# Attention output projection of a hybrid encoder layer as two runs of eight output blocks, six of its 16 units by seven products

## The chip, the cores and the metric

The kernel runs on one core of one Trainium2 chip. The metric is the device time of one execution in microseconds (us), taken as the median of several runs. The engines are TensorE (PE in the profile; PEld is its loading of the stationary operand), VectorE (DVE), ScalarE (ACT), GpSimd (POOL, hardly used here) and SyncE (SP, whose queue issues the loads).

## The reference

One encoder layer over 256 tokens of width 2048, in float32. What matters here:

```python
n = rms_norm(h, norm_mix_w)
u = n @ w_in                  # latents | SSD z, xBC, dt_fwd, dt_bwd | g_attn, g_ssd
# attention: 16 heads, V_HEAD_DIM 128
p = softmax(scores * scale);  o = p @ v
attn_out = o.reshape(256, 2048) @ w_o_attn          # the output projection
# SSD: dt = softplus(dt_raw + dt_bias); a_cs = cumsum(-exp(a_log) * dt) in chunks of 128
mixed = sigmoid(g_attn) * attn_out + sigmoid(g_ssd) * ssd_out
h = h + mixed @ w_out
h = h + conv_ffn(rms_norm(h))
out = rms_norm(h)
```

## The kernel before

Every float32 product is made of three TensorE products: both operands are split into a rounded part and a rest (H and L), and HH, HL and LH are summed in PSUM.

Weights come in *units* of 16 blocks of 128x128, 1 MB. A unit is loaded into one of three raw buffers (`load`, L119), split in halves by ScalarE (`wh`, L195) and VectorE (`wl`, L196) into one of five pairs of buffers, and multiplied. `jobs` is the list of units in program order; `at(slot, fn)` hangs a smaller step, such as one step of an attention head, on the unit with that number. From this a scheduler fixes the order of the instructions on each engine; an instruction waits on semaphores for its inputs and for free buffers. Loads go out on SP's queue in the order of the units. Working tiles come from a pool of 29 pages (`page`) and one of 18 smaller ones (`p1`). PSUM has four banks for sums of units (`gpsum`, named g) and four for the rest (`spsum`, named s).

The stages that matter, in order:

- **Attention.** A string of letters gives the order of the units: R and V and QK for the heads, g for a unit of the attention's gate (`ga_job`). Each QK unit serves two heads, and each head then goes through `att1` (scores in PSUM, their maximum on VectorE L670, exponential on ScalarE L674, reciprocal and scaling of p on VectorE L676 and L678), `att2` (four transposes of p on TensorE, L686, copied into pT by ScalarE and VectorE) and `att3` (p times v, written as oT by L702 and L703). Fourteen of the 16 gate units stand here.
- **Output projection.** `quad` (L241) makes four units for each of four groups of four column blocks. A unit is 24 matmuls of 128x512 (L257, L258, L259), four loads of 256 KB, and two halves to split. At the end of a group `oa_evac` (L717) multiplies the gate with the sum straight from PSUM and the group is stored to `mixD`. The last two gate units stand between the first units, and the steps of dt (`dt_softplus` L495, `dt_tokens`, `dt_cumsum`, `dt_rows`) hang on slots 41 to 50 in this stage.
- **SSD start** and its eight groups, then the **SSD output projection**, which `os_run` (L921) does in two runs of eight column blocks with 16 units each. Four units of the first run and six of the second are *seven-product* units: a 2x2 block product by seven block products instead of eight (M1 to M7). Such a unit needs sums of weight blocks (`split_seven`, L152, on VectorE), sums of the left operand (`sums_of`, L892), and at the end of a run the combination of the seven sums (`inner` L939 and `outer` L950). M1, M5, M6 and M7 lie in s banks, the others in g banks.
- Output of the mixer and the convolutional MLP, which the change does not touch; the latter has its own seven-product units and calls `act_sums`.

Of the kernel before, what the change touches and what calls it, by code (L numbers as in the profile page):

```python
# [11 lines left out]
AF = mybir.ActivationFunctionType  # L12
ALU = mybir.AluOpType
AX = mybir.AxisListType

P = 128
# [48 lines left out]
def tile_bidir_hybrid_layer(ctx: ExitStack, tc, xT, pos, vec, cst, w_in, w_r, w_v, w_qk, w_oa,  # L65
# [11 lines left out]
    def page(shape, dt=F32, name="pg"):  # L77
        return pp.tile(shape, dt, tag="pg", bufs=NPG, name=name)
# [10 lines left out]
    def f32(ap):  # L89
        return ap.bitcast(F32)  # L90
# [150 lines left out]
    def quad(src, q, kt, get, evac):  # L241


        cell = {}

        def unit(u):
            def mm(h, n, wh, wl):
                if u == 0 and h == 0:
                    cell["ps"] = [gpsum([P, 512]), gpsum([P, 512])]
                wH, wL = (w.rearrange("p (k m) c -> p k (m c)", k=2) for w in (wh, wl))  # L250
                for kk in range(2):
                    k = 4 * u + 2 * h + kk
                    x = get(k)
                    for t in range(2):
                        ts = slice(t * P, (t + 1) * P)
                        ps = cell["ps"][t]
                        pe.matmul(ps, lhsT=x[:, 0, ts], rhs=wH[:, kk, :], start=k == 0, stop=False)  # L257
                        pe.matmul(ps, lhsT=x[:, 0, ts], rhs=wL[:, kk, :], start=False, stop=False)  # L258
                        pe.matmul(ps, lhsT=x[:, 1, ts], rhs=wH[:, kk, :], start=False, stop=k == kt - 1)  # L259

            def ev():
                if 4 * u + 4 == kt:
                    for t in range(2):
                        evac(q, t, cell["ps"][t])
            j = Job([src(4 * q + m)[:, 4 * u:4 * u + 4, :] for m in range(4)], 16, mm, ev)
            j.quad = True
            return j
        return [unit(u) for u in range(kt // 4)]
# [88 lines left out]
    def pair(st, k):  # L357
        return st[k // 2][:, :, k % 2, :]
# [333 lines left out]
    def att3(h):  # L692
        t = att.pop((h, "T"))
        vh, vl = vv[h // 4]
        d = slice((h % 4) * P, (h % 4) * P + P)
        ps = spsum([P, S])
        for kb in range(2):
            mm3(ps, vh[:, kb, d], vl[:, kb, d], t[:, 0, kb, :], t[:, 1, kb, :], kb == 0, kb == 1)
        if h % 2 == 0:
            oT[h // 2] = page([P, 2, 2, S], F32R, name="oT")  # L700
        o = oT[h // 2]
        act.activation(o[:, 0, h % 2, :], ps, AF.Copy)  # L702
        dve.tensor_sub(o[:, 1, h % 2, :], ps, f32(o[:, 0, h % 2, :]))  # L703


    ta, ts_ = {}, {}

    def gate_evac(store):
# [5 lines left out]

    mixD = dr.tile([4, P, 2, 512], F32, name="mixD")

    def oa_evac(q, t, ps):  # L717
        g = ta[q]
        dve.scalar_tensor_tensor(g[:, t, :], g[:, t, :], 1.0, ps, ALU.add, ALU.mult)
        if t == 1:  # L720
            nc.sync.dma_start(mixD[q], g)


    class Grp:
# [189 lines left out]
    def seven_left(pr, st, nm):  # L914
        if nm in ("A11", "A12", "A22"):
            k, t = int(nm[2]) - 1, int(nm[1]) - 1
            return [pr[:, i, k, t * P:(t + 1) * P] for i in range(2)]
        i = ("W1", "R", "N4", "N2").index(nm)
        return [a[:, i, :] for a in st]

    def os_run(n, order, cap):  # L921


        M, left, res = {}, {}, {}
        for kp, sv in order:
            for nm, c in ([(nm, 1) for hh in SEVEN for nm, _ in hh] if sv
                          else [(nm, 2) for nm in ("M2", "M3", "M4", "P22")]):
                left[nm] = left.get(nm, 0) + 3 * c
        total = dict(left)
        sevens_left = [sum(sv for _, sv in order)]  # L930

        def add(nm, aH, aL, bH, bL):
            if nm not in M:
                M[nm] = spsum([P, 512]) if nm in ("M1", "M5", "M6", "M7") else gpsum([P, 512])
            for x, w in ((aH, bH), (aH, bL), (aL, bH)):
                pe.matmul(M[nm], lhsT=x, rhs=w, start=left[nm] == total[nm], stop=left[nm] == 1)  # L936
                left[nm] -= 1

        def inner():  # L939
            c, v = page([P, 2, 512], name="m15"), page([P, 2, 512], name="vx")  # L940
            m1, m5, V, X = c[:, 0, :], c[:, 1, :], v[:, 0, :], v[:, 1, :]
            act.activation(m1, M["M1"], AF.Copy)
            act.activation(m5, M["M5"], AF.Copy)
            dve.tensor_sub(V, M["M6"], m1)
            dve.tensor_add(X, M["M7"], V)
            dve.tensor_add(V, V, m5)
            dve.tensor_add(m5, X, m5)
            res.update({(0, 0): m1, (1, 0): X, (0, 1): V, (1, 1): m5})

        def outer(h):  # L950
            for t, nm in ((0, ("M2", "M3")[h]), (1, ("M4", "P22")[h])):
                o = res[t, h]
                dve.tensor_tensor(o, M[nm], o, ALU.subtract if nm == "M4" else ALU.add)
            cap(n, h, res)

        def unit(i, kp, sv):
            def mm(h, nb, wh, wl):
                if sv:
                    for a, (nm, lf) in enumerate(SEVEN[h]):
                        aH, aL = seven_left(yHL[kp], yS[kp], lf)  # L960
                        add(nm, aH, aL, *(w[:, 4 * a:4 * a + 4, :].rearrange("p m c -> p (m c)")
                                          for w in (wh, wl)))
                else:
                    wH, wL = (w.rearrange("p (k m) c -> p k (m c)", k=2) for w in (wh, wl))
                    for k in range(2):
                        for t, nm in ((0, ("M2", "M3")[h]), (1, ("M4", "P22")[h])):
                            aH, aL = (yHL[kp][:, j, k, t * P:(t + 1) * P] for j in range(2))
                            add(nm, aH, aL, wH[:, k, :], wL[:, k, :])
                    if i == len(order) - 1:
                        outer(h)  # L970

            def ev():
                if sv:
                    sevens_left[0] -= 1
                    if sevens_left[0] == 0:
                        inner()
            kh, kk = kp // 8, 2 * kp % 16
            j = Job(w_os[8 * n:8 * n + 8, kh, :, kk:kk + 2, :].rearrange("m p k c -> p m (k c)"), 16, mm, ev)
            j.wide, j.seven = True, sv
            if sv:  # L980
                j.nh = 4
            return j
        assert not order[-1][1] and not order[0][1]
        return [unit(i, kp, sv) for i, (kp, sv) in enumerate(order)]
# [78 lines left out]
    def val_ev(m):  # L1063
        def ev(ps):
            o = conv3(ps, NFF + m)
            dve.tensor_mul(o, o, gv.pop(m))
            if m % 2 == 0:
                aHL[m // 2] = page([P, 2, 2, S], F32R, name="aHL")
            hi, lo = aHL[m // 2][:, 0, m % 2, :], aHL[m // 2][:, 1, m % 2, :]
            act.activation(hi, o, AF.Copy)  # L1070
            dve.tensor_sub(lo, o, f32(hi))  # L1071
            if m % 2 == 0:
                even[0] = o
            elif m // 2 in sevens:
                act_sums(m // 2, even[0], o)
        return ev


# [2 lines left out]
    NU = 5  # L1081
    sevens = {8 * p + u for p in range(2) for u in range(NU)}

    def act_sums(kp, e, o):
        w = page([P, 4, P], name="asum")
        sums_of([w[:, i, :] for i in range(4)], e, o)
        t = page([P, 2, 4, P], F32R, name="aS")
        hilo(t[:, 0], t[:, 1], w)
        aS[kp] = t[:, 0], t[:, 1]

    def seven_jobs(p):
        cell = {}
# [117 lines left out]
    def at(slot, fn, *a):  # L1210
        late.append((slot, lambda: fn(*a)))
# [24 lines left out]
    for m in range(7, 11):  # L1236
        at(m, rope_steps, 12 if m < 10 else 99)
    at(15, kr_rope)
    at(41, dt_softplus)
    at(46, dt_tokens)  # L1240
    at(48, dt_cumsum)
    at(50, dt_rows)

    ga = [0]
    ga_units = [u for q in range(4) for u in quad(lambda m: w_in[10 + m], q, 16, lambda k: pair(nHL, k),
# [4 lines left out]
    def ga_job():  # L1250
        jobs.append(ga_units[ga[0]])
        ga[0] += 1
# [33 lines left out]
            at(s + 3 + b, att2, 2 * i + b)  # L1286
            at(s + 4 + b, att3, 2 * i + b)

    for it in "g R0 g g g V0 QK0 g QK1 V1 QK2 g QK3 V2 R1 g QK4 g QK5 V3 QK6 g QK7 g g g g g".split():
        if it == "g":  # L1290
            ga_job()
        elif it[0] == "R":
            R(int(it[1]))
        elif it[0] == "V":
            Vj(int(it[1]))
        else:
            QK(int(it[2]))
    for q in range(4):
        for u in quad(lambda m: w_oa[m], q, 16, lambda k: pair(oT, k), oa_evac):
            jobs.append(u)  # L1300
            if ga[0] < 16:
                ga_job()
    gs = [0]

    def gate_s(n):
# [40 lines left out]
        at(b + i, ssd_sums, g)  # L1346
    for n in range(2):
        assert sorted(kp for kp, _ in runs[n]) == list(range(16))
        jobs += os_run(n, runs[n], cap)
    at(b + 17, ssd_r)  # L1350
    for q in range(2):
        at(b + 17 + q, mix_load, q)
# [245 lines left out]
```

## Time and profile before

| | us |
|---|---|
| median of 3 runs | 1944.09 |
| lowest and highest | 1944.06, 1944.98 |
| the profiled execution's own time | 1944.84 |
| its span, first to last instruction | 1943.1 |

| engine | busy us | share of the span | instructions |
|---|---|---|---|
| TensorE | 1928.8 | 99% | 10948 |
| VectorE | 1556.6 | 80% | 2583 |
| ScalarE | 1243.5 | 64% | 1975 |

A row of a group of instructions gives line, engine, operation, the tiles written and read, shapes and count, then busy time in us and the mean of one in ns, then the idle time ahead of it and what ended it. A row of the timeline gives start and duration in us, then the same names, and in square brackets the idle time before it. A row of a stretch gives the busy time of each engine in it with the number of its instructions, the clock that TensorE was granted (1.00 is full), and the share and rate of DMA. Attention's crowded part is 108 to 257 us, the output projection 257 to 363 us, the start of the SSD stage 363 to 435 us, the SSD output projection 935 to 1098 us.

### The profile page before, as it was taken

Reading aid. Unit: us, or ns where it says so; the run is one execution under the profiler, and the core shown is the slowest. Engines: PE = TensorE matmul, PEld = TensorE weight load, DVE = VectorE, ACT = ScalarE, POOL = GpSimd, SP = SyncE. Lnnn points to the kernel's source line nnn. Section 1 sums busy time; section 2 is a strip of 40 time slices with the busy share of each in tenths; the row PEclk is TensorE's granted clock in tenths of the full one; section 3 lists DMA queues with packets and bytes.
Section 4 is the critical chain, followed back from the end, with each engine's and each line's share of the span. In section 5 each row is a group of like instructions: output and inputs, shape, how many; then the busy total and the mean of one; then the engine's idle time right before and its main releaser. Section 6 shows DMA issues by size and latency. Waiting matters only on the chain.

```text
span 1943.1 us, 28860 instructions
## 1 busy us (share of the span) xinstructions
PE 1928.8 (99%) x10948; PEld 1689.8 (87%) x10948; DVE 1556.6 (80%) x2583; ACT 1243.5 (64%) x1975; POOL 16.2 (1%) x36
## 2 busy tenths in 40 slices
PE   9999999999999999999999999999999999999997
PEld 8899988888888888888888888888888888888887
DVE  7887765779779779779898876888887888977775
ACT  6566543788888887878665554665555565545563
POOL 0200000000000000000000000000000000000000
PEclk9999999999999999999999999999999999999998
DMA  7644456765665665665566675545555555564543
GB/s 283 203 158 159 131 174 218 252 225 174 217 220 173 214 233 168 208 237 170 172 198 204 209 256 176 193 177 197 183 185 217 177 205 182 182 209 179 206 163 125
DMA packets 118906, 379.55 MB, mean 195 GB/s; under 512 B 9712, under 2 KB 53168, under 8 KB 90864
## 3 DMA queue, kind: packets, MB, share of 16 engines
q1 hardware_dynamic: 116976, 375.09, 56.6%
q0 software_dynamic: 1024, 1.54, 0.3%
q8 instruction: 86, 1.41, 0.3%
q10 hardware_dynamic: 768, 1.09, 0.2%
q14 instruction: 52, 0.43, 0.1%
HBM read 372.08 MB, written 4.42 MB: 194 GB/s over the span
## 4 chain that ended last, share of the span: by engine, by line
PE 97%; DVE 1%; ACT 1%; DMA 1%; issue 0%; SPq 0%; DVEq 0%; ACTq 0%
PE g L222 41%; PE g L229 21%; PE g L936 7%; PE g L257 5%; PE g L258 4%; PE g L259 4%; PE s L936 1%; PE g L201 1%; PE g L203 1%; PE g L202 1%; PE s L222 1%; PE s L841 1%; PE s L850 1%; PE s L201 0%; PE s L203 0%; PE s L202 0%
## 5 line engine op out<-in xcount | busy, mean ns | idle before, releaser
L196 DVE TENSOR_TENSOR wl<-raw,wh 128x1024 fp32r<-128x1024 f32 (+1 forms) x634 | 754.5, 1201 | 207.4 <-ACT wh L195 127.7
L195 ACT ACTIVATE wh<-raw 128x1024 fp32r<-128x1024 f32 (+1 forms) x634 | 654.9, 1039 | 317.0 <-PE g L222 109.6
L222 PE MATMUL g<-xHL,wh 128*128 128x512 f32 x1424 | 341.7, 392 | 0.2 <-DVE cu L272 0.2
L222 PE MATMUL g<-hHL,wh 128*128 128x512 f32 x1408 | 327.8, 390 | 0.0
L222 PEld LDWEIGHTS g<-xHL,wh 128*128 128x128 f32 x1424 | 262.5, 188 | 52.1 <-PE s L203 0.4
L222 PEld LDWEIGHTS g<-hHL,wh 128*128 128x128 f32 x1408 | 261.4, 188 | 52.4
L229 PEld LDWEIGHTS g<-xHL,wl 128*128 128x128 f32 x1424 | 182.6, 191 | 6.9
L229 PE MATMUL g<-xHL,wl 128*128 128x256 f32 x1424 | 184.7, 283 | 0.0
L229 PEld LDWEIGHTS g<-hHL,wl 128*128 128x128 f32 x1408 | 174.8, 192 | 3.4
L229 PE MATMUL g<-hHL,wl 128*128 128x256 f32 x1408 | 176.0, 283 | 0.0
L1053 DVE SCALAR_TENSOR_TENSOR uc<-u,V,uc 128x255 f32<-128x255 f32 x176 | 84.6, 481 | 56.8 <-ACT uc L1051 55.3
L222 PE MATMUL g<-aHL,wh 128*128 128x512 f32 x532 | 126.8, 391 | 0.5 <-DVE aHL L1071 0.5
L1051 ACT ACTIVATE uc<-u,V 128x256 f32<-128x256 f32 x88 | 52.3, 594 | 116.5 <-DVE u L279 116.5
L936 PE MATMUL g<-wh,yHL 128*128 128x512 f32 x392 | 125.0, 390 | 0.0
L222 PEld LDWEIGHTS g<-aHL,wh 128*128 128x128 f32 x532 | 98.3, 188 | 20.8 <-DVE aHL L1071 1.4
L257 PE MATMUL g<-wh,xHL 128*128 128x512 f32 x256 | 100.3, 392 | 0.0
L258 PE MATMUL g<-wl,xHL 128*128 128x512 f32 x256 | 100.0, 390 | 0.0
L259 PE MATMUL g<-wh,xHL 128*128 128x512 f32 x256 | 99.6, 389 | 0.0
L936 PEld LDWEIGHTS g<-wh,yHL 128*128 128x128 f32 x392 | 73.6, 188 | 15.2
L147 ACT ACTIVATE wh<-raw 128x1024 fp32r<-128x1024 f32 (+1 forms) x80 | 56.9, 733 | 38.0 <-PE g L936 13.3
L936 PE MATMUL g<-wl,yHL 128*128 128x512 f32 x196 | 76.3, 389 | 0.0
L229 PEld LDWEIGHTS g<-aHL,wl 128*128 128x128 f32 x532 | 67.9, 191 | 2.4
(375 smaller groups left out, 2881.2 us busy)
## 6 DMA issues: line engine op xcount, KB each, us to landing
raw<-in_w_in SPq DMA_DIRECT2D x88, 1024.0 KB, 4.9
raw<-in_w_up SPq DMA_DIRECT2D x88, 1024.0 KB, 4.9
raw<-in_w_in SPq DMA_DIRECT2D x128, 256.0 KB, 3.8
raw<-in_w_os SPq DMA_DIRECT2D x32, 1024.0 KB, 6.0
raw<-in_w_dn SPq DMA_DIRECT2D x26, 1024.0 KB, 5.0
raw<-in_w_oa SPq DMA_DIRECT2D x64, 256.0 KB, 4.1
FB<-acsD SPq DMA_DIRECT2D x32, 512.0 KB, 7.5
raw<-in_w_out SPq DMA_DIRECT2D x12, 1024.0 KB, 5.0
```

The source lines that it names most:

```text
L147: act.activation(wh, v, AF.Copy)
L195: act.activation(vh, r, AF.Copy)
L196: dve.tensor_sub(vl, r, f32(vh))
L201: pe.matmul(ps, lhsT=wH, rhs=xH, start=first, stop=False)
L222: pe.matmul(ps, lhsT=wh[:, b, :], rhs=x, start=k == 0, stop=False)
L229: pe.matmul(cell["ps"][:, 0, :], lhsT=wl[:, b, :], rhs=get(k)[:, 0, :], start=False, stop=k == ktot - 1)
L257: pe.matmul(ps, lhsT=x[:, 0, ts], rhs=wH[:, kk, :], start=k == 0, stop=False)
L258: pe.matmul(ps, lhsT=x[:, 0, ts], rhs=wL[:, kk, :], start=False, stop=False)
L259: pe.matmul(ps, lhsT=x[:, 1, ts], rhs=wH[:, kk, :], start=False, stop=k == kt - 1)
L936: pe.matmul(M[nm], lhsT=x, rhs=w, start=left[nm] == total[nm], stop=left[nm] == 1)
L1051: act.activation(o, u, AF.Identity, scale=vcol("fcw", 88 + cb), bias=vcol("fcb", cb))
L1053: dve.scalar_tensor_tensor(o[:, a], u[:, b], vcol("fcw", k * 88 + cb), o[:, a], ALU.mult, ALU.add)
```

## The change

The output projection becomes two runs of eight column blocks with eight units each, by the function that the SSD output projection uses (`os_run`, now `mixed_run`, which takes the source of its weights and its left operands as arguments). In each run the units of head pairs 4, 5 and 6 are seven-product units: the order of a run is 0, S4, 1, S5, 2, S6, 3, 7. That makes 366 matmuls of 128x512 instead of 384, and 16 loads of 1 MB instead of 64 of 256 KB. For heads 8 to 13 `att3` first copies the PSUM tile into a page `of` by one more ScalarE step, and every second head VectorE adds up the four sums that the seven-product units need and splits them (`act_sums`). The end of a run is `inner`, two `outer`, and `oa_cap`, which multiplies the gates and stores two groups to `mixD`.

All 16 gate units now stand in the attention string, one more before V1 and one more before V3. `dt_softplus` hangs on slot 20, the V1 unit, instead of 41; the other dt steps on 36 to 38, at the end of the string.

```diff
+        if h // 2 in oa_sevens:
+            if h % 2 == 0:
+                of[h // 2] = page([P, 2, S], name="of")
+            f = of[h // 2][:, h % 2, :]
+            act.activation(f, ps, AF.Copy)
+        else:
+            f = ps
+        act.activation(o[:, 0, h % 2, :], f, AF.Copy)
+        dve.tensor_sub(o[:, 1, h % 2, :], f, f32(o[:, 0, h % 2, :]))
+        if h // 2 in oa_sevens and h % 2:
+            f = of.pop(h // 2)
+            act_sums(oS, h // 2, f[:, 0, :], f[:, 1, :])
+    oa_sevens, of, oS = {4, 5, 6}, {}, {}
...
-    def oa_evac(q, t, ps):
-        g = ta[q]
-        dve.scalar_tensor_tensor(g[:, t, :], g[:, t, :], 1.0, ps, ALU.add, ALU.mult)
-        if t == 1:
-            nc.sync.dma_start(mixD[q], g)
+    def oa_cap(n, h, res):
+        g = ta[2 * n + h]
+        for t in range(2):
+            dve.scalar_tensor_tensor(g[:, t, :], g[:, t, :], 1.0, res[t, h], ALU.add, ALU.mult)
+        nc.sync.dma_start(mixD[2 * n + h], g)
...
-    at(41, dt_softplus)
-    at(46, dt_tokens)
-    at(48, dt_cumsum)
-    at(50, dt_rows)
+    at(20, dt_softplus)
+    at(36, dt_tokens)
+    at(37, dt_cumsum)
+    at(38, dt_rows)
...
-    for it in "g R0 g g g V0 QK0 g QK1 V1 QK2 g QK3 V2 R1 g QK4 g QK5 V3 QK6 g QK7 g g g g g".split():
+    for it in "g R0 g g g V0 QK0 g QK1 g V1 QK2 g QK3 V2 R1 g QK4 g QK5 g V3 QK6 g QK7 g g g g g".split():
...
-    for q in range(4):
-        for u in quad(lambda m: w_oa[m], q, 16, lambda k: pair(oT, k), oa_evac):
-            jobs.append(u)
-            if ga[0] < 16:
-                ga_job()
+    order = [(int(w.lstrip("S")), w[0] == "S") for w in "0 S4 1 S5 2 S6 3 7".split()]
+    for n in range(2):
+        jobs += mixed_run(n, order, lambda m, k: w_oa[m:m + 8, :, k:k + 2, :].rearrange("m p k c -> p m (k c)"),
+                          oT, oS, oa_cap)
```

How the order of instructions moves, at three places on VectorE. Names of tiles: p, pT and oT are a head's tiles, sm its maxima and sums, s and g are PSUM banks, wl and vl low parts.

First, attention beside the units QK0 to QK2, behind the scaling of one head's p. Before:

```order
L678 TENSOR_SCALAR p<-p,sm 128x256 x2
L196 TENSOR_TENSOR wl<-raw,wh 128x4x2x128
L633 TENSOR_TENSOR vl<-g,vh 128x512 x2
L703 TENSOR_TENSOR oT<-s,oT 128x256
L196 TENSOR_TENSOR wl<-raw,wh 128x1024
L689 TENSOR_TENSOR pT<-s,pT 128x512
L670 TENSOR_REDUCE sm<-s 128x2
L671 TENSOR_SCALAR sm<-sm 128x2
L676 RECIPROCAL sm<-sm 128x2
L678 TENSOR_SCALAR p<-p,sm 128x256 x2
```

After:

```order
L678 TENSOR_SCALAR p<-p,sm 128x256 x2
L501 TENSOR_SCALAR t<-e 128x256
L502 RECIPROCAL t<-t 128x256
L710 TENSOR_TENSOR oT<-s,oT 128x256
L503 TENSOR_TENSOR t<-t,e 128x256
L689 TENSOR_TENSOR pT<-s,pT 128x512
L504 TENSOR_TENSOR t_1369<-t 128x256
L670 TENSOR_REDUCE sm<-s 128x2
L506 TENSOR_SCALAR o<-t_1369 128x256
L671 TENSOR_SCALAR sm<-sm 128x2
L196 TENSOR_TENSOR wl<-raw,wh 128x4x2x128
L508 TENSOR_TENSOR o<-o,t_1369 128x256
```

The softplus (L501 to L508, `t` and `o`) now stands step by step between the steps of the next heads, and one split of a unit stands between a head's maximum and its reciprocal; the split of V1 (`vl`) came here before and comes later now.

Second, the change from one group or run of the output projection to the next. Before:

```order
L196 TENSOR_TENSOR wl<-raw,wh 128x4x2x128
L719 SCALAR_TENSOR_TENSOR gate<-gate,g 128x512 x2
L196 TENSOR_TENSOR wl<-raw,wh 128x4x2x128 x8
L719 SCALAR_TENSOR_TENSOR gate<-gate,g 128x512 x2
L196 TENSOR_TENSOR wl<-raw,wh 128x4x2x128
```

After:

```order
L964 TENSOR_TENSOR m15_3252<-g_3017,m15_3252 128x512
L964 TENSOR_TENSOR vx_3253<-g_3021,vx_3253 128x512
L731 SCALAR_TENSOR_TENSOR gate_1033<-gate_1033,m15_3252 128x512
L731 SCALAR_TENSOR_TENSOR gate_1033<-gate_1033,vx_3253 128x512
L148 TENSOR_TENSOR wl_3321<-T13_3300,wh_3320 128x1024
L167 TENSOR_TENSOR raw_3294<-T13_3300,raw_3294 128x4x128
L964 TENSOR_TENSOR vx_3253<-g_3035,vx_3253 128x512
L168 TENSOR_TENSOR raw_3294<-raw_3294 128x4x128
L964 TENSOR_TENSOR m15_3252<-g_3039,m15_3252 128x512
L731 SCALAR_TENSOR_TENSOR gate_1985<-gate_1985,vx_3253 128x512
L731 SCALAR_TENSOR_TENSOR gate_1985<-gate_1985,m15_3252 128x512
```

Before, only splits of halves stand here, with the two gate products of a group from time to time. Now the last sums of the first run (`outer`, L964, reading four g banks) and the gate products (L731) are mixed with the split of the next run's first seven-product unit (L148, L167, L168).

Third, the start of the SSD stage, ahead of its first convolution (`cu`, `bcf`, `bcL`). Before:

```order
L196 TENSOR_TENSOR wl<-raw,wh 128x1024 x4
L719 SCALAR_TENSOR_TENSOR gate<-gate,g 128x512 x2
L196 TENSOR_TENSOR wl<-raw,wh 128x1024 x3
L272 TENSOR_TENSOR cu<-cu,g 128x256
L736 SCALAR_TENSOR_TENSOR bcf<-cu,V,bcf 128x254
L736 SCALAR_TENSOR_TENSOR bcf<-cu,V,bcf 128x255 x2
L736 SCALAR_TENSOR_TENSOR bcf<-cu,V,bcf 128x254
L196 TENSOR_TENSOR wl<-raw,wh 128x1024 x2
L745 TENSOR_TENSOR bcL<-bcf,bcH 128x256
```

After:

```order
L964 TENSOR_TENSOR m_3594<-g,m_3594 128x512
L964 TENSOR_TENSOR vx<-g,vx 128x512
L731 SCALAR_TENSOR_TENSOR gate<-gate,m_3594 128x512
L731 SCALAR_TENSOR_TENSOR gate<-gate,vx 128x512
L196 TENSOR_TENSOR wl<-raw,wh 128x1024
L964 TENSOR_TENSOR vx<-g,vx 128x512
L964 TENSOR_TENSOR m_3594<-g,m_3594 128x512
L731 SCALAR_TENSOR_TENSOR gate<-gate,vx 128x512
L731 SCALAR_TENSOR_TENSOR gate<-gate,m_3594 128x512
L797 SCALAR_TENSOR_TENSOR FB<-FB,acs 128x128
L196 TENSOR_TENSOR wl<-raw,wh 128x1024 x2
L272 TENSOR_TENSOR cu<-cu,g 128x256
```

The last group's two gate products before are now the end of the second run, four sums and four gate products, with a decay step (`FB`) behind.

More of the change, by code (lines that the diff above doesn't have):

```diff
@@ L701, in att3 @@
         o = oT[h // 2]
-        act.activation(o[:, 0, h % 2, :], ps, AF.Copy)
-        dve.tensor_sub(o[:, 1, h % 2, :], ps, f32(o[:, 0, h % 2, :]))
+        if h // 2 in oa_sevens:
[11 more added lines that the diff above has]
+    oa_sevens, of, oS = {4, 5, 6}, {}, {}
     ta, ts_ = {}, {}
@@ L919, in seven_left, with mixed_run @@
         return [a[:, i, :] for a in st]
-    def os_run(n, order, cap):
+    def mixed_run(n, order, src, st, sm, cap):
         M, left, res = {}, {}, {}
@@ L959, in mm @@
                     for a, (nm, lf) in enumerate(SEVEN[h]):
-                        aH, aL = seven_left(yHL[kp], yS[kp], lf)
+                        aH, aL = seven_left(st[kp], sm[kp], lf)
                         add(nm, aH, aL, *(w[:, 4 * a:4 * a + 4, :].rearrange("p m c -> p (m c)")
@@ L966, in mm @@
                         for t, nm in ((0, ("M2", "M3")[h]), (1, ("M4", "P22")[h])):
-                            aH, aL = (yHL[kp][:, j, k, t * P:(t + 1) * P] for j in range(2))
+                            aH, aL = (st[kp][:, j, k, t * P:(t + 1) * P] for j in range(2))
                             add(nm, aH, aL, wH[:, k, :], wL[:, k, :])
@@ L976, in ev @@
                         inner()
-            kh, kk = kp // 8, 2 * kp % 16
-            j = Job(w_os[8 * n:8 * n + 8, kh, :, kk:kk + 2, :].rearrange("m p k c -> p m (k c)"), 16, mm, ev)
+            j = Job(src(8 * n, 2 * kp), 16, mm, ev)
             j.wide, j.seven = True, sv
@@ L1074, in ev @@
             elif m // 2 in sevens:
-                act_sums(m // 2, even[0], o)
+                act_sums(aS, m // 2, even[0], o)
         return ev
@@ L1082, in tile_bidir_hybrid_layer, with act_sums @@
     sevens = {8 * p + u for p in range(2) for u in range(NU)}
-    def act_sums(kp, e, o):
+    def act_sums(st, kp, e, o):
         w = page([P, 4, P], name="asum")
@@ L1088, in act_sums @@
         hilo(t[:, 0], t[:, 1], w)
-        aS[kp] = t[:, 0], t[:, 1]
+        st[kp] = t[:, 0], t[:, 1]
     def seven_jobs(p):
@@ L1348, in tile_bidir_hybrid_layer @@
         assert sorted(kp for kp, _ in runs[n]) == list(range(16))
-        jobs += os_run(n, runs[n], cap)
+        jobs += mixed_run(n, runs[n], lambda m, k: w_os[m:m + 8, k // 16, :, k % 16:k % 16 + 2, :].rearrange(
+            "m p k c -> p m (k c)"), yHL, yS, cap)
     at(b + 17, ssd_r)
```

## The prediction

> **What bounds the kernel now.** I read the page first, then the busy time by stage, then the timeline of each engine.
>
> ```profile
> span 1943.1 us, 28860 instructions
> ...
> PE 1928.8 (99%) x10948; PEld 1689.8 (87%) x10948; DVE 1556.6 (80%) x2583; ACT 1243.5 (64%) x1975; POOL 16.2 (1%) x36
> ...
> PE 97%; DVE 1%; ACT 1%; DMA 1%; issue 0%; SPq 0%; DVEq 0%; ACTq 0%
> ```
>
> TensorE is busy for 99% of the span and carries 97% of the chain that ended last. So a matmul taken away shortens the span by its issue step, and a matmul that has to wait lengthens it by the whole wait. The stages that the change touches, in order of the rows: attention, out-projection, start of the SSD stage; the fourth is the SSD out-projection, which already runs in the form that the change brings.
>
> ```profile
> core 0: us, PE busy (x) PEld busy (x) DVE busy (x) ACT busy (x) POOL busy (x), PEclk, DMA share, GB/s
> 108.00:257.00 149.00, 149.00 (x991) 137.31 (x991) 109.96 (x186) 86.38 (x169) 3.92 (x8) 1.00 0.45 150
> 257.00:363.00 106.00, 106.00 (x479) 87.92 (x478) 64.58 (x90) 52.59 (x73) 0.00 (x0) 1.00 0.68 225
> 363.00:435.00 72.00, 72.00 (x403) 63.04 (x402) 54.22 (x93) 53.54 (x89) 0.00 (x0) 1.00 0.64 217
> 935.00:1098.00 163.00, 163.00 (x763) 135.31 (x762) 144.38 (x188) 95.32 (x120) 0.00 (x0) 1.00 0.66 198
> ```
>
> TensorE is busy all the time in each, at a granted clock of 1.00. VectorE has 39 us spare in attention, 41 us in the out-projection, 18 us in the SSD start. The last row matters as a precedent: two runs of 16 units, ten of the 32 by seven products, load VectorE to 144.38 of 163 us (89%), and TensorE still loses nothing.
>
> **What goes.** Six of 32 out-projection units take seven products instead of eight, 21 matmuls for 24: 6 x 3 = 18 matmuls of 128x512 fewer, 366 for 384. Their step:
>
> ```profile
> 89.81 0.39 PE L257 MATMUL g<-wh,xHL 128*128 128x512 f32 x1
> 90.03 0.39 PE L258 MATMUL g<-wl,xHL 128*128 128x512 f32 x1
> 90.26 0.39 PE L259 MATMUL g<-wh,xHL 128*128 128x512 f32 x1
> ```
> ```profile
> 257.00:363.00 106.00, 88.39 (x384) 71.85 (x384) 0.42 (x1) 0.37 (x1) 1.00 0.68 225
> ```
>
> The starts lie 0.225 us apart, although each is shown as 0.39 us long (they overlap); the second row, of the oT tile alone, gives 88.39 / 384 = 0.230 with the tails of its blocks. I take 0.227. The saving is 18 x 0.227 = 4.1 us, between 18 x 0.225 = 4.05 and 18 x 0.230 = 4.14. All other matmuls, those of the two moved gate units and of the dt steps among them, only change place: 0 on TensorE.
>
> The Trainium skill (TensorE: Matmul & The Clock Gate, Back-to-back issue gap) gives about 216 ns for an isolated 512-wide step and about 131 ns sustained. By its second figure the saving would be 18 x 0.131 = 2.4 us and the time about 1.7 us higher than I forecast; 384 matmuls in 88.39 us contradict it here, so I give it no more than 0.01.
>
> **What is added on VectorE in the out-projection.** Its prices are from the rows below, of 257 to 363 us and of 935 to 1098 us.
>
> ```profile
> L196 DVE TENSOR_TENSOR wl<-raw,wh 128x1024 fp32r<-128x1024 f32 x38 | 46.5, 1223 | 41.1 <-ACT wh L195 41.1
> L719 DVE SCALAR_TENSOR_TENSOR gate<-gate,g 128x512 f32<-128x512 f32 x7 | 4.5, 682 | 0.0
> L508 DVE TENSOR_TENSOR o<-o,t 128x256 f32<-128x256 f32 x8 | 3.4, 425 | 0.2
> L509 DVE TENSOR_SCALAR o<-o 128x256 f32<-128x256 f32 x8 | 2.3, 291 | 0.2
> L502 DVE RECIPROCAL t<-t 128x256 f32<-128x256 f32 x1 | 1.8, 1755 | 0.0
> L703 DVE TENSOR_TENSOR oT<-s,oT 128x256 fp32r<-128x256 f32 x1 | 0.4, 418 | 0.0
> L545 DVE TENSOR_TENSOR wsuf<-w,dtok 128x64 f32<-128x64 f32 x2 | 0.4, 222 | 0.4 <-ACT w L542 0.4
> ```
> ```profile
> L148 DVE TENSOR_TENSOR wl<-raw,wh 128x512 fp32r<-128x512 f32 x29 | 18.7, 686 | 2.3 <-ACT wh L147 2.2
> L148 DVE TENSOR_TENSOR wl<-T,wh 128x1024 fp32r<-128x1024 f32 x10 | 12.2, 1220 | 0.3 <-ACT wh L147 0.3
> L161 DVE TENSOR_TENSOR T<-raw 128x512 f32<-128x512 f32 x10 | 6.9, 688 | 5.8 <-DMA raw<-in_w_os 5.8
> L953 DVE TENSOR_TENSOR vx<-g,vx 128x512 f32<-128x512 f32 x2 | 1.4, 684 | 0.0
> ```
>
> A plain unit splits two halves: 2 x 1.22 = 2.4 us. A seven-product unit takes 2 x 1.22 + 3 x 0.686 + 4 x 0.688 = 7.25 us, so six add 6 x (7.25 - 2.44) = 28.9. At a run's end stand four `inner` and four `outer` steps of 0.684 beside four of 0.682 that were there as L719: 5.5 us more a run. The stage becomes 10 x 2.44 + 6 x 7.25 + one run's end of 8.2 + about 2.5 of attention's tail and decay steps = 78.6 us, against 366 x 0.227 = 83.1 us of matmuls: 95%, against 89% in the precedent. A seven-product unit with the plain one behind it is 9.7 us of VectorE beside 45 x 0.227 = 10.2 us of TensorE; the five pairs of split buffers let VectorE run ahead, so I cost this at nothing. At the change of runs the second run's first M3 matmul needs a bank that VectorE frees with the last `outer` steps: by my walk along the changed order that comes from 0.5 us ahead to 0.9 us late. I take 0.
>
> ScalarE stands at 52.59 of 106 us; six seven-product units add one 512-wide and a half copy each, the runs four, no stall. The loads:
>
> ```profile
> raw<-in_w_os SPq DMA_DIRECT2D x32, 1024.0 KB, 6.0
> ...
> raw<-in_w_oa SPq DMA_DIRECT2D x64, 256.0 KB, 4.1
> ```
>
> Sixteen 1 MB loads replace 64 of 256 KB, in the form of the SSD out-projection, where one lands 6.0 us after issue while a plain unit keeps TensorE 24 x 0.227 = 5.4 us. Three raw buffers cover two units, 10.9 us: 0. The mixD stores now go out in pairs behind loads issued earlier on SP's queue; nobody reads them until the SSD out-projection.
>
> **What is moved into attention.** Two gate units (48 x 0.227 = 10.9 us of TensorE, 4.9 of VectorE), the softplus, the three small dt steps, and new sums for three head pairs. The softplus is 8 x 0.425 + 8 x 0.291 + 1.755 = 7.5 us, and seven more steps of the same shape, between 0.29 and 0.43 each, 2.6: 10.1 us. The sums are three times four subtractions of 128x128 (between the rows of 0.22 and 0.42, so 0.28) and one split of 0.686: 5.4. With the four small steps of the cumulative sum (0.222 each, 0.9) VectorE gets 21.3 us more and goes from 109.96 of 149 to 131 of 160 us, 82%. On average that fits. What counts is the latency chain of each head:
>
> ```profile
> 118.07 0.62 DVE L678 TENSOR_SCALAR p<-p,sm 128x256 f32<-128x256 f32 x2
> 120.35 0.60 PE L686 MATMUL s<-CT,p 128*128 128x128 f32 x4
> ...
> 133.65 0.17 DVE L676 RECIPROCAL sm<-sm 128x2 f32<-128x2 f32 x1 [1.15 <-ACT p L674]
> 133.85 0.62 DVE L678 TENSOR_SCALAR p<-p,sm 128x256 f32<-128x256 f32 x2
> ...
> 218.19 0.62 DVE L678 TENSOR_SCALAR p<-p,sm 128x256 f32<-128x256 f32 x2
> 218.99 0.60 PE L686 MATMUL s<-CT,p 128*128 128x128 f32 x4
> ```
>
> A head's p is scaled 118.07 + 0.62 = 118.69, and TensorE transposes it at 120.35: 1.66 us spare. One head, at 218.81 and 218.99, has 0.18. VectorE waits 1.15 us inside a head for the exponentials; softplus steps can fill such holes, which is why not all of the 10.1 us delays anything. In the changed order the worst interval is that between two heads beside QK1 and QK2: 24 VectorE rows of 12.4 us by durations. Neighbours that don't depend on each other start about 0.08 us closer than their durations say:
>
> ```profile
> 277.52 1.23 DVE L196 TENSOR_TENSOR wl<-raw,wh 128x1024 fp32r<-128x1024 f32 x1 [1.49 <-ACT wh L195]
> 278.66 0.29 DVE L501 TENSOR_SCALAR t<-e 128x256 f32<-128x256 f32 x1
> ```
>
> Here 1.14 us lie between the starts for a duration of 1.23. So the 24 rows take 10.5 us. TensorE has 64 matmuls of 256 columns at 0.12 (the step from 385.05 to 385.17 in the rows of the next part), 5 at 0.227 and four transposes within 0.6, together 9.3 us, between the same two transposes. The shortfall, 1.2 us, meets a slack of about 1 that is left there: 0.3 us of stall. I add 0.1 and 0.4 for two other heads whose scaling now stands behind a sum or a gate unit's split, and 0.3 where pT waits for a page, the 29 pages now being held by oT, `of` and the sums together. Sum 1.1 us. The bounds are 0 (all of it in holes) and VectorE's 21.3 us in line beside 10.9 us of added matmuls, with a head's slack used once: 21.3 - 10.9 - 1.7 = 8.7; 1.1 is nearer to the low end because the steps are spread over several heads, each with its own slack and holes.
>
> **What arrives at the SSD stage.** The second run's end (8.2 us) and some decay steps now stand in the SSD start, where before only two 0.68 us steps stood, and two more table loads of ScalarE.
>
> ```profile
> 381.53 0.42 DVE L745 TENSOR_TENSOR bcL<-bcf,bcH 128x256 fp32r<-128x256 f32 x1
> ```
> ```profile
> 385.05 0.28 PE L202 MATMUL s<-bcL,bcH 128*128 128x256 f32 x1
> 385.17 0.28 PE L203 MATMUL s<-bcH,bcL 128*128 128x256 f32 x1
> ```
> ```profile
> 373.21 1.28 ACT L737 ACT_TABLE_LOAD   x1
> ```
>
> The first product that needs bcL starts 385.05 - 381.95 = 3.1 us after it is there. About 10 us come to VectorE where it has 18 of 72 spare, and 2 x 1.28 us to ScalarE; by my walk 0.5 us of the 3.1 is left. I take 0, with bounds 0 and 2.
>
> **The sum.** -4.1 + 1.1 + 0 = -3.0 us. The profiled span of 1943.1 stands in an execution of 1944.84, 1.74 around it, 0.75 above the median of 1944.09. So the profiled time becomes 1941.8 and the median 1941.1; I write 1941.0.
>
> **Rivals.** *All of the gain is kept* (1940.0): for it speaks the precedent and that TensorE has no idle row in these stages; against it the head with 0.18 us and the crowded interval. *The out-projection or its end binds* (1944.0): at 95% VectorE falls behind, one M3 bank costs 0.9, the SSD start 2.0, and the 1.1 of attention takes the rest of the 4.1. It decides where a pair of units takes VectorE longer than 10.2 us, now 9.7. *The softplus holds the heads' p* (slower, 1948.7): its dependent steps stand one by one between the steps of four or five heads, and TensorE waits at their transposes. The upper bound above, 8.7, less 4.1 gives +4.6. It decides where stalls in attention pass 4.1 + 3.9 = 8 us; against it speak the 1.15 us holes and the 29 us of VectorE that remain idle there. Here a rule of the Trainium skill could add to it (TensorE: Matmul & The Clock Gate, HAM oscillation — how this bites in real kernels): a TensorE pause over about 3.4 us drops the clock; no row here pauses so long and the clock stays 1.00.
>
> **Numbers.** A measurement of this kernel tells about 0.2%, 3.9 us, from no change. Forecast (1940.2 to 1943) 0.50; all kept, under 1940.2, 0.22; out-projection binds (1943 to 1947.9) 0.12; softplus holds the heads (above) 0.16. So faster 0.22, same 0.62, slower 0.16. The likeliest case's own range is 1940.2 to 1943.0. The range 1939.6 to 1946.5 leaves out the softplus case and the ends of the others.
>
> **What would show it.** 366 matmuls of the out-projection (tiles oT and aS) in about 83 to 84 us; idle of TensorE before L686 in attention of about 1 us in total (none: all kept; over 8: the softplus); VectorE near 95% of the out-projection with no wait of TensorE for split buffers or banks there; bcL still ahead of its product. Wrong would be a stall of over 1 us at the change of runs, or a loss in stages where the order is the same.

## The result and the profile after

| | median, us | runs | profiled execution, us | its span, us |
|---|---|---|---|---|
| before | 1944.77 (1943.97 to 1945.64) | 16 | 1944.84 | 1943.1 |
| changed | 1941.21 (1940.05 to 1942.45) | 16 | 1940.05 | 1938.3 |

The ratio is 0.9982, with a 95% interval of 0.9975 to 0.9988: 3.6 us faster, between 2.3 and 4.9, and just inside the 0.2% that the prediction took as no change. The profiled execution is the fastest of its 16, so its span lies 4.8 us below that of before while the medians differ by 3.6.

The page of the changed kernel, its span, engines and chain:

```profile
span 1938.3 us, 28840 instructions
...
PE 1925.5 (99%) x10930; PEld 1687.0 (87%) x10930; DVE 1592.0 (82%) x2656; ACT 1262.0 (65%) x2008; POOL 16.2 (1%) x36
...
PE 96%; DVE 2%; ACT 1%; DMA 1%; issue 0%; SPq 0%; DVEq 0%
```

TensorE has 10948 - 10930 = 18 matmuls less and VectorE 73 instructions more. TensorE's timeline gives a stretch that holds all of its work that the change moves or takes away: from the first gate matmul of attention to the first matmul of the SSD stage. Before:

```profile
68.22 0.47 PE L257 MATMUL g<-wh,xHL 128*128 128x512 f32 x1
...
362.69 0.62 PE L222 MATMUL g<-xHL,wh 128*128 128x512 f32 x2
```

The changed kernel, with the first matmul of the projection between them:

```profile
67.90 0.47 PE L257 MATMUL g<-wh,xHL 128*128 128x512 f32 x1
...
276.10 0.39 PE L947 MATMUL g<-wh,oT 128*128 128x512 f32 x1
...
359.11 0.39 PE L222 MATMUL g<-xHL,wh 128*128 128x512 f32 x1
```

The stretch is 362.69 - 68.22 = 294.47 us before and 359.11 - 67.90 = 291.21 after: -3.26, close to the difference of the medians. 359.11 - 276.10 = 83.01 us for 366 matmuls is 0.2268 each, so in the projection TensorE waits for nothing. Eighteen matmuls at this step are worth 4.08 us; the stretch became 3.26 us shorter, so 0.82 us is lost, and as the projection has no waits, it is lost in attention. The same two parts by busy time of the engines (TensorE, weight loads, VectorE, ScalarE):

```profile
67.90:276.10 208.20, 208.07 (x1305) 187.38 (x1304) 162.71 (x294) 123.64 (x228) 13.89 (x28) 1.00 0.50 160
276.10:359.10 83.00, 83.00 (x367) 68.71 (x366) 73.19 (x96) 53.01 (x76) 0.00 (x0) 1.00 0.71 237
```

VectorE is busy for 73.19 of 83.00 us in the projection, 88%. It is not spread evenly: in the next rows, two pieces of which the second begins ahead of the change of runs (315 to 323 us on VectorE), it has 10 us spare in the first 40 and nearly nothing in the 30 that follow.

```profile
270.00:310.00 40.00, 40.00 (x181) 33.24 (x180) 30.20 (x36) 23.43 (x30) 0.00 (x0) 1.00 0.58 180
310.00:340.00 30.00, 30.00 (x134) 24.80 (x133) 29.75 (x39) 16.45 (x22) 0.00 (x0) 1.00 0.75 245
```

The rest of the span's difference is not in this stretch: 0.32 us stand at the start (68.22 against 67.90), 0.14 us behind TensorE's last matmul, and 1.08 us between the first SSD matmul and that last one. There the order of the instructions is the same from early in the SSD stage on, and the waits differ from one execution to the next (last section).

### The profile page after: what moved, and what is told of

Same layout as the page of the kernel before. It is cut to its first block, busy times and chain, and to the rows that moved or that the text cites. A ratio compares the mean times of both kernels' runs of the same rounds, so it can differ in the third digit from the quotient of the medians.

```text
span 1938.3 us, 28840 instructions
## 1 busy us (share of the span) xinstructions
PE 1925.5 (99%) x10930; PEld 1687.0 (87%) x10930; DVE 1592.0 (82%) x2656; ACT 1262.0 (65%) x2008; POOL 16.2 (1%) x36
## 4 chain that ended last, share of the span: by engine, by line
PE 96%; DVE 2%; ACT 1%; DMA 1%; issue 0%; SPq 0%; DVEq 0%
PE g L222 40%; PE g L229 21%; PE g L947 11%; PE g L257 3%; PE g L258 3%; PE g L259 3%; PE s L947 2%; PE g L201 1%; PE g L203 1%; PE g L202 1%; PE s L222 1%; PE s L852 1%; PE s L861 1%; PE s L201 0%; DVE wl L196 0%; PE s L203 0%
## 5 line engine op out<-in xcount | busy, mean ns | idle before, releaser
L196 DVE TENSOR_TENSOR wl<-raw,wh 128x1024 fp32r<-128x1024 f32 (+1 forms) x622 | 740.0, 1202 | 169.2 <-ACT wh L195 85.6
L148 DVE TENSOR_TENSOR wl<-raw,wh 128x1024 fp32r<-128x1024 f32 (+1 forms) x104 | 82.6, 822 | 8.3 <-ACT wh L147 4.8
```

Of the source, the lines that this page charges most:

```text
L148: dve.tensor_sub(wl, v, f32(wh))
L196: dve.tensor_sub(vl, r, f32(vh))
```

## The experiments

Each is read by its medians and by the stretch of its profiled execution; two of them ("one run") have a single execution and are read by their traces alone. "Attention" reaches from the first gate matmul to the first matmul of the projection, "projection" from there to the first SSD matmul. "Waits" is the time of the projection less 0.2267 us for each of its matmuls. The medians of before, run beside them, were 1944.82 (for the first four experiments of the table), 1945.27 (the next four) and 1945.11 (the last three).

| kernel | matmuls | attention, us | projection, us | its waits, us | stretch, us | median, us | ratio to before (95%) |
|---|---|---|---|---|---|---|---|
| before | 384 | 194.40 | 100.07 | with gate units and dt steps | 294.47 | 1944.77 | |
| changed | 366 | 208.20 | 83.01 | 0.0 | 291.21 | 1941.21 | 0.9982 (0.9975 to 0.9988) |
| one seven | 378 | 207.96 | 85.68 | 0.0 | 293.64 | 1943.38 | 0.9992 (0.9983 to 1.0001) |
| dt between runs | 366 | 206.10 | 85.17 | 2.2, with dt steps | 291.27 | 1941.69 | 0.9983 (0.9974 to 0.9992) |
| attention only | 384 | 207.52 | 87.04 | 0.0 | 294.56 | 1945.92 | 1.0005 (0.9997 to 1.0014) |
| four sevens | 360 | 208.49 | 83.91 | 2.3 | 292.39 | 1944.88 | 1.0002 (0.9993 to 1.0011) |
| polynomial twice | 366 | 208.09 | 83.22 | 0.2 | 291.31 | 1941.85 | 0.9983 (0.9974 to 0.9992) |
| sums later | 366 | 207.95 | 83.02 | 0.0 | 290.97 | 1940.93 | 0.9978 (0.9969 to 0.9987) |
| four, then three | 363 | 208.53 | 83.47 | 1.2 | 292.00 | 1942.92 | 0.9987 (0.9978 to 0.9997) |
| four, earlier | 360 | 208.54 | 84.55 | 2.9 | 293.09 | 1945.47 (one run) | |
| banks first | 366 | 207.97 | 82.96 | 0.0 | 290.93 | 1941.05 | 0.9979 (0.9970 to 0.9988) |
| four, then three, banks first | 363 | 209.16 | 83.30 | 1.0 | 292.46 | 1942.64 | 0.9988 (0.9979 to 0.9996) |
| four, banks first | 360 | 208.54 | 83.85 | 2.2 | 292.39 | 1944.54 (one run) | |

**Is the gain the matmuls taken away?** One seven-product unit a run, and the attention part by itself:

```diff
-    order = ... "0 S4 1 S5 2 S6 3 7"        # oa_sevens = {4, 5, 6}
+    order = ... "0 S4 1 5 2 6 3 7"          # oa_sevens = {4}
```

> One seven-product unit per run (head pair 4) instead of three, the rest as in the changed kernel: 378 matmuls in the output projection instead of 366. Theory A (the gain is the issue time of the matmuls taken away, nothing else): 12 x 0.227 = 2.7 us come back, less some 0.2 us because two of three sums leave attention; about 1943.7 us against 1941.2, and from the first attention gate matmul to the first SSD matmul 293.7 us instead of 291.2. Theory B (the gain is from the form: 1 MB loads, two runs, the dt steps out of the projection): no change from 1941.2.

```diff
 # the kernel before, its projection by quad
-    at(41, dt_softplus); at(46, dt_tokens); at(48, dt_cumsum); at(50, dt_rows)
+    at(20, dt_softplus); at(36, dt_tokens); at(37, dt_cumsum); at(38, dt_rows)
-    "g R0 g g g V0 QK0 g QK1 V1 ... QK5 V3 QK6 g QK7 g g g g g"
+    "g R0 g g g V0 QK0 g QK1 g V1 ... QK5 g V3 QK6 g QK7 g g g g g"
```

> The kernel before with only its attention changed: 16 gate units in the string, softplus and dt steps on the slots of the changed kernel; the output projection stays with 384 matmuls. Theory A (the crowded attention costs about 0.8 us, part of it by the sums, which are not here): 0.4 to 0.8 us over before, 1945.2 to 1945.6. Theory B (no cost, the holes take everything): 1944.8. Theory C (the softplus holds the heads' p): over 1948.

Theory A holds in the first. With 378 matmuls the projection is 85.68 - 83.01 = 2.67 us longer (12 x 0.227 = 2.72), and the median 2.2 us higher; with 384, in the old form with its 256 KB loads, 87.04 - 83.01 = 4.03 us. The form by itself, wide loads and two runs, gives nothing that shows. In the second kernel the stretch is theory B's: the attention part costs 294.56 - 294.47 = 0.09 us, not the 0.4 to 0.8 of theory A, so in this execution gate units and softplus move for almost nothing. Its median lies 1.1 us over before, above what theory A allowed, with an interval that includes no change; in its profiled execution 1.0 us of the difference stands between the first SSD matmul and TensorE's last (1572.04 us against 1571.03), behind all that was moved. Theory C is out.

**How much cover has the softplus?**

```diff
+        for _ in range(2):
             dve.tensor_scalar(o, t2, ...)
             for k in range(n - 2, -1, -1): ...
```

> The changed kernel with the polynomial of the softplus (17 VectorE steps, 6.0 us by their durations) worked out twice in attention; the result is the same. Theory A (VectorE's holes and each head's slack still cover it): from the first gate matmul to the first SSD matmul 291.2 becomes 291.2 to 292.5 us. Theory B (attention's cover is used up by the change): nearly all of it shows, 295 to 297 us, and the time rises to 1945 to 1947.

VectorE's groups of this kernel in attention show the 32 steps of the doubled loop (a multiplication and an addition for each of two times eight terms; lines are one higher here):

```profile
L509 DVE TENSOR_TENSOR o<-o,t 128x256 f32<-128x256 f32 x16 | 6.7, 420 | 0.1
L510 DVE TENSOR_SCALAR o<-o 128x256 f32<-128x256 f32 x16 | 4.6, 290 | 0.1
```

Some 6 us more on VectorE make the stretch 0.10 us longer (attention itself is 0.11 shorter, the projection 0.21 longer). Theory A, at its lower end: VectorE's holes take a second polynomial. That they take the first as well is what the kernel before showed with its attention changed.

**Could the dt steps have stayed in the projection?** During a run M1, M5, M6 and M7 hold the four s banks from the first seven-product unit to `inner`, and M2, M3, M4 and P22 the four g banks, as the code of `add` shows. So the steps of dt that use an s bank, and gate units, which hold two g banks through four units, must stand outside a run; a run with them inside was not tried. At the change of runs the s banks are free for a while:

```diff
-    at(20, dt_softplus); at(36, dt_tokens); at(37, dt_cumsum); at(38, dt_rows)
+    at(41, dt_softplus); at(46, dt_tokens); at(47, dt_cumsum); at(48, dt_rows)
```

> The softplus goes back into the output projection (first run), the token, cumsum and row steps to the change of runs, where the four s banks are free. Theory A (VectorE is occupied there by the distance between starts, 71 of 83.5 us, so 10 us more still fit, 97%): the attention waits of about 0.8 us mostly go, the projection waits 0 to 1.5 us; 1940.4 to 1942. Theory B (occupied as the durations add up, 78.6 of 83 us): 78.6 + 10.1 = 88.7 us do not fit; 5 to 6 us slower than the changed kernel, 1946 to 1947.

The stretch is 291.27, 0.06 us from the changed kernel's: 2.1 us leave attention and 2.16 arrive in the projection. Most of it is the steps' own 18 matmuls, 1.74 us from start to start in the changed kernel; so of attention's 0.82 us of waits at most 0.4 left with them, and theory A's "mostly go" did not come. VectorE's ten us more do fit into the projection, as theory A says; theory B, by durations, is out. The row of the projection (its engines in the order of the rows above) has VectorE busy for 81.47 of 85.20 us, 96%, and no wait of TensorE is recorded in it:

```profile
274.20:359.40 85.20, 85.20 (x386) 70.60 (x385) 81.47 (x124) 55.65 (x85) 0.00 (x0) 1.00 0.70 235
```

Here, too, the place of the softplus is worth nothing either way.

**Where is the limit on seven-product units?**

```diff
-    order = ... "0 S4 1 S5 2 S6 3 7"
+    order = ... "0 S4 1 S5 S3 2 S6 7"       # oa_sevens = {3, 4, 5, 6}
```

> A fourth seven-product unit per run (head pair 3, order 0 S4 1 S5 S3 2 S6 7): 360 matmuls, and one more set of sums in attention. Theory A (VectorE by distance between starts: 71 + 2 x 4.4 = 80 of 82 us, fits): 6 x 0.227 = 1.4 us less, at most 0.4 us more in attention; 1939.8 to 1940.3. Theory B (by durations: 78.6 + 9.6 = 88 of 82 us): VectorE binds the projection, some 5 us slower than the changed kernel, 1946.

Neither theory had the size: 1.36 us of matmuls go, 2.3 us of waits come in the projection, and the median is back at that of before. The waits of TensorE in 270 to 362 us of this kernel, and then in 362 to 900 us, where before and the changed kernel have 0.2 us alone:

```profile
PE g L947 <- DVE m L964: 0.9, 1, 0.9
PE s L947 <- ACT wh L147: 0.2, 1, 0.2
```
```profile
PE g L222 <- DVE cu L272: 1.0, 2, 0.8
PE s L202 <- DVE bcL L756: 0.4, 1, 0.4
```

The largest is at the change of runs, for the `outer` sum (L964) that frees a g bank; 1.2 us more are lost in the SSD stage, where the scheduler's order also came out differently. In the changed kernel the same sum and its user stand so:

```profile
319.57 0.69 DVE L964 TENSOR_TENSOR vx<-g,vx 128x512 f32<-128x512 f32 x1
```
```profile
320.30 0.39 PE L947 MATMUL s<-wh,oT 128*128 128x512 f32 x1
320.52 0.40 PE L947 MATMUL g<-wh,oT 128*128 128x512 f32 x1
```

M3's bank is free at 320.26 and used again at 320.52: 0.26 us to spare. Two kernels try whether the seven-product unit's position, or the run it is in, decides:

```diff
+    orders = "0 S3 S4 1 S5 S6 2 7", "0 S4 1 S5 2 S6 3 7"     # four, then three
+    order = "0 S3 S4 1 S5 S6 2 7"                            # four, earlier
+    # oa_sevens = {3, 4, 5, 6} in both
```

> Four seven-product units in the first run only, early (0 S3 S4 1 S5 S6 2 7), three in the second as in the changed kernel: 363 matmuls. Theory A (VectorE has room in the first run, it is full only from the change of runs on): 0.7 us less on TensorE, at most 0.2 more in attention, so the stretch is 290.5 to 290.8 us. Theory B (the first run's load arrives at the change of runs and its bank is late): a wait of 0.5 to 2 us there, 291.2 to 293 us.

> Four seven-product units in both runs as in the kernel with four, but early in each run (0 S3 S4 1 S5 S6 2 7). Theory A (the position of the last seven-product unit right ahead of the run's end made the bank late): the 1.1 us wait at the change of runs goes, the stretch is 290.0 to 291 us. Theory B (VectorE is simply full in the projection): 2 us of waits again, 292 to 293 us.

Both stretches are theory B's (292.00, and 293.09, just above its 293). With four in the first run alone, TensorE waits at the change of runs:

```profile
320.71 0.39 PE L947 MATMUL s<-wl,oT 128*128 128x512 f32 x1
321.69 0.50 PE L947 MATMUL g<-wh,oT 128*128 128x512 f32 x1 [0.59 <-DVE vx L964]
```

and VectorE has the sum that it waits for behind two gate products, a split of 1.22 us and an addition:

```profile
317.41 0.68 DVE L964 TENSOR_TENSOR vx<-g,vx 128x512 f32<-128x512 f32 x1
318.01 0.68 DVE L731 SCALAR_TENSOR_TENSOR gate<-gate,m 128x512 f32<-128x512 f32 x1
318.61 0.69 DVE L731 SCALAR_TENSOR_TENSOR gate<-gate,vx 128x512 f32<-128x512 f32 x1
319.21 1.22 DVE L148 TENSOR_TENSOR wl<-T,wh 128x1024 fp32r<-128x1024 f32 x1
320.35 0.69 DVE L167 TENSOR_TENSOR raw<-T,raw 128x512 f32<-128x512 f32 x1
320.95 0.68 DVE L964 TENSOR_TENSOR vx<-g,vx 128x512 f32<-128x512 f32 x1
```

There is no hole in these rows. The kernel with four early in both runs has this wait too (0.78 us longer than a step, at 320.64), but not all of its 2.9 us are VectorE's. A wait nearly as long, in the second run, is for a split on ScalarE:

```profile
345.22 0.39 PE L947 MATMUL g<-wh,oT 128*128 128x512 f32 x1
346.19 0.73 PE L947 MATMUL s<-wh,aS 128*128 128x512 f32 x2 [0.58 <-ACT wh L147]
```
```profile
343.31 1.87 ACT L796 ACTIVATE FB<-FB,nacs 128x128 f32<-128x128 f32 x6 [0.70 <-DMA FB<-acsD]
345.09 1.04 ACT L147 ACTIVATE wh<-T 128x1024 fp32r<-128x1024 f32 x1
```
```profile
343.79 0.68 DVE L162 TENSOR_TENSOR T<-raw 128x512 f32<-128x512 f32 x1
```

VectorE has the sum T ready at 344.47, and ScalarE begins its split at 345.09, behind six decay steps of the SSD stage that had themselves waited for a load. Without them it could have begun some 0.6 us earlier; a kernel with them moved was not tried.

For the wait at the change of runs the gate products were put behind all four sums:

```diff
 def oa_cap(n, h, res):
+    if h == 0:
+        return
+    for h in range(2): ...      # both pairs of gate products, then both stores
```

> Four seven-product units in the first run, three in the second, with the sums that free the banks ahead of the gate products. Theory A (the wait of 0.75 us at the change of runs is a wait for the M3 bank behind two gate products of 0.6 us each): the wait goes, the stretch falls from 292.0 to 291.0 to 291.3. Theory B (VectorE is late as a whole by then): the wait moves to the next half or the next unit, the stretch stays at 291.8 to 292.2.

> Four seven-product units in both runs, early, with the sums that free the banks ahead of the gate products. Theory A (only the bank was late): the first of the waits (0.78 us) goes, the stretch falls from 293.1 to 292.3. Theory B (VectorE full): the sum of the waits in the projection stays at about 2.9 us, 293.0.

With four, then three, the waits in the projection go from 1.2 to 1.0 us, in several small pieces. That is theory B: the wait moves on, and the only one long enough to be recorded there (0.2 us) is for the fourth sum, `m`. Its order on VectorE still has the split of 1.22 us and the addition between the second sum and the third; an order with these behind all four was not tried. Its stretch is 0.46 us longer than without the reordering, since in that execution attention lost 0.63 us more, 0.55 of it at 108 us, in a wait for VectorE's low part of V (L633) that the other kernels with four do not have at that place. With four in both runs theory A has the amount, 293.09 to 292.39, but only the bank's part: 2.2 us of waits stay. In the orders tried, three a run is what the projection carries. VectorE's total alone does not set this limit: it is busy for 81.47 of 85.20 us with the dt steps between the runs, without a recorded wait, and for 77.07 of 83.90 with four sevens, with 2.3 us of waits:

```profile
276.50:360.40 83.90, 82.70 (x361) 67.29 (x360) 77.07 (x100) 50.75 (x72) 0.00 (x0) 1.00 0.66 219
```

What counts is which step stands ahead of the one that TensorE needs next.

**What do the sums cost in attention?**

```diff
         if h // 2 in oa_sevens and h % 2:
-            act_sums(oS, h // 2, f[:, 0, :], f[:, 1, :])
+    for i, kp in enumerate((4, 5, 6)):
+        at(39 + 2 * i, oa_sums, kp)      # oa_sums: the same act_sums, its definition left out here
```

> The changed kernel with the three sets of left-operand sums taken out of attention and put between the first units of the output projection (the pages of the copies are held longer). Theory A (in attention the sums and copies cost the 0.7 us by which the changed kernel is behind the one with the attention part alone): the stretch from the first gate matmul to the first SSD matmul falls by 0.3 to 0.7 us to about 290.7. Theory B (the projection has no room for 5 us more of VectorE, its bank at the change of runs is free only 0.26 us ahead): 0.5 to 3 us longer there, total 291.5 to 294.

The stretch falls by 0.24 us, a little less than theory A's 0.3, and the projection takes the sums without a wait. So the sums' time on VectorE is the smaller part of the 0.7 us: attention goes from 208.20 to 207.95, and the kernel before with its attention changed has 207.52. What is left, 0.43 us, is still there with the copies alone: 0.23 us is the same wait for a page as in the changed kernel (next section), and 0.2 us stands at a head's transposes at 239 us, whose cause was not traced. Together with the gate products behind the sums:

> The changed kernel with two reorderings on VectorE: the sums between the first units of the projection (as in the run before), and at a run's end both pairs of sums that free the g banks ahead of all four gate products (instead of two, two, two, two). Theory A (the bank of M3 is then free some 1.2 us earlier, which the projection with three seven-product units does not need, and the sums give 0.24 us): the stretch from the first gate matmul to the first SSD matmul is 290.9 to 291.0 us, time 1941.0, the same as the changed kernel. Theory B (the margin at the change of runs matters in executions other than the profiled one): the median falls below 1940.5.

290.93 us and a median of 1941.05: theory A. This is the shortest stretch of all, 0.28 us under the changed kernel's, but the medians of the two (1941.05 and 1941.21, with 1.3 and 2.4 us between the lowest and highest of their runs) can't be told apart, and a version that measurably beats the changed kernel was not found.

## Why the prediction was right

Forecast 1941.0 us, range 1939.6 to 1946.5; measured 1941.21. The mechanism was right: 18 steps of TensorE less, a part lost in attention, nothing lost in the projection or at the start of the SSD stage. That the time is met to 0.2 us is partly luck. The forecast took 3.1 us off a median of 1944.09 from three runs; with 16 runs that median is 0.68 higher, 1944.77, and the change is 0.5 larger, 3.56, and the two differences nearly cancel. Point by point:

- **The saving.** 18 x 0.227 = 4.1 us was predicted; the slopes of the experiments are 2.67 us for 12 and 4.03 for 18. The step of 0.227 from the timeline holds to 0.005, and 83.01 us for 366 is 0.2268. The figure of 131 ns that the Trainium skill gives for sustained work (TensorE: Matmul & The Clock Gate, Back-to-back issue gap) does not hold in these runs. The prediction's "six of 32" units is a slip: there are 16, ten plain and six with seven products, and its sums go by these.
- **The waits in attention.** Predicted 1.1 us, measured 0.82 over the whole stretch. Part of it is found where it was looked for. A head's p scaled late: at 246.49 TensorE's matmul is followed by the transposes at 247.00 and not 0.227 later, 0.28 us lost, and moving the sums away takes it off. The page that pT waits for: ScalarE writes pT at 233.20 after 1.69 us of idleness, ended by TensorE's last matmul on a tile whose page it takes over, and the two steps of TensorE around its first matmul on this pT (from 233.60 to 233.85 and on to 234.08) are 0.23 us longer than their 0.12. The steps ahead of the transposes (L686) lost about 0.5 us in all, half of the 1 us that was named as the sign.

```profile
246.49 0.39 PE L257 MATMUL g<-wh,xHL 128*128 128x512 f32 x1
247.00 0.30 PE L686 MATMUL s<-CT,p 128*128 128x128 f32 x1
```
```profile
246.50 0.62 DVE L678 TENSOR_SCALAR p<-p,sm 128x256 f32<-128x256 f32 x2
```
```profile
233.20 0.60 ACT L688 ACTIVATE pT<-s 128x512 fp32r<-128x512 f32 x1 [1.69 <-PE g L202]
```
```profile
233.60 0.28 PE L202 MATMUL g<-latL,wh 128*128 128x256 f32 x1
233.85 0.39 PE L201 MATMUL s<-pT,vh 128*128 128x256 f32 x1
234.08 0.28 PE L201 MATMUL s<-qk 128*128 128x256 f32 x1
```

  The 0.3 us that I gave to the interval crowded by the softplus is the part that did not come as argued: softplus and gate units together cost 0.09 without the sums, and doubling the polynomial 0.10, so the steps fill holes to a far larger extent than the walk along the order allowed. Of the 0.82, some 0.7 came with the copies and the sums, for which the prediction had 0.8 at most (0.5 for two heads late behind a sum or a gate unit's split, and 0.3 for the page). The upper bound of 8.7 us, VectorE's work added in line, was the wrong picture altogether.
- **The projection at nothing.** No wait there, as costed. The load was predicted as 78.6 us by durations; the groups of VectorE in the projection add up to 79.5, but the row above shows 73.19 busy, because neighbours overlap by some 0.07 us for each of 96 instructions. 88%, not 95%, is the number to compare with TensorE's time. The 0.5 us ahead to 0.9 late at the change of runs became 0.26 ahead.
- **The SSD start at nothing.** 0.5 us of the 3.1 was to be left; the first bcL for the product is complete at 380.14 + 0.42 = 380.56 and used at 381.47, so 0.9 is left. TensorE's recorded waits from 362 to 900 us are the same 0.2 us before and after.

```profile
380.14 0.42 DVE L756 TENSOR_TENSOR bcL<-bcf,bcH 128x256 fp32r<-128x256 f32 x1 [1.75 <-ACT bcH L755]
```
```profile
381.47 0.28 PE L202 MATMUL s<-bcL,bcH 128*128 128x256 f32 x1
```

- **The rivals.** All kept: out, by 0.82 us in the stretch; the medians alone could not tell, since their interval of 2.3 to 4.9 us holds the full 4.1. The projection or its end binds: out at three seven-product units, and at four the waits there (2.2 to 2.9 us in both runs) pass the matmuls saved, though one of them was ScalarE's. The softplus holds the heads: out, by the doubled polynomial and by the attention part alone.

The sum of 3.0 us against 3.26 in the stretch is off by the attention term alone. The median's 3.56 lies 0.3 further, well within its interval.

## What to carry to other kernels

Where TensorE never waits, a reformulation is worth its matmuls times their measured step, and the question is whether the engine that pays still has holes where the payment falls. A busy share does not answer it: VectorE was 88% busy over the projection and 99% around the change of runs without making TensorE wait, 96% with the dt steps in it, again without, and 92% with four sevens and 2.3 us of waits. So look at the single step that TensorE needs next, how long ahead it is done, and what stands before it in its engine's order. Work with slack on both sides (the softplus here) can be moved freely, so the place to look for a loss is what holds a bank or a page. Compare a stretch between two fixed matmuls when a change is of the size of the spread between executions.

## What was not expected of the hardware

Executions of the same kernel differ by about 0.1% (1943.97 to 1945.64 us before, 1940.05 to 1942.45 changed), and in the profiles much of the difference stands in one place: waits of TensorE in the MLP behind its seven-product units, for `aHL` from VectorE. Before had the first row, the kernel with the dt steps between runs the second, the changed kernel no such wait:

```profile
PE g L222 <- DVE aHL L1071: 0.5, 1, 0.5
```
```profile
PE g L222 <- DVE aHL L1081: 1.6, 1, 1.6
```

From the first SSD matmul to TensorE's last, the profiled executions of kernels whose order of instructions in the MLP is the same took 1569.95 us (changed), 1570.33 (sums later), 1570.70 (banks first) and 1572.13 (dt between runs), and that of before 1571.03. The changed kernel's is the shortest of all, which is why its whole span would flatter it. What makes VectorE late there in one execution and not in the next was not looked into.
